# Hybrid encoder layer on one core: the router gathers part of the first expert's rows early, and makes the first weights later

## The chip, the core and the metric

One core of one Trainium2 chip runs the whole program in one launch. The time is the device time of that core in microseconds (us); lower is better.

## What is computed

The layer has one mixer (a state-space group and an attention group, joined by an output projection), a layer norm, and a mixture of 16 experts with another layer norm. The change lies between the first norm and the second expert. Cut to what matters (512 tokens, width 1024, experts 512 wide, 4 groups of 4 experts, 2 experts per token):

```python
h = layer_norm(alpha * x + mix, ln1_g, ln1_b)
g_val, g_idx = top_k(softmax(h @ rg_w + rg_b), 1)
e_logits = (einsum('td,gde->tge', h, re_w) + re_b)[g_idx]
e_val, e_idx = top_k(softmax(e_logits), 2)
weights = g_val * e_val / sum(e_val)
for e in range(16):
    act = silu(h @ w_gate[e]) * (h @ w_up[e])
    out = out + combine[:, e:e + 1] * (act @ w_down[e])
y = layer_norm(alpha * h + out, ln2_g, ln2_b)
```

## The kernel before

The 512 tokens are four tiles of 128 rows. PE (TensorE) runs nearly all the time; ACT (ScalarE), DVE (VectorE) and POOL (GpSimd) feed it and empty its results. PE's instructions keep the order of the code, and inside the router's block (from line 1305) those of DVE, ACT and POOL do as well; outside that block a scheduler sets the order on the three. Each engine takes its own queue in order, so that an instruction that waits holds all that stand behind it. SP issues the weights' DMAs, POOL those that gather and scatter rows.

**Router.** For each tile t `proj_half` finishes the output projection in two halves of 12 matmuls (line 805); `norm_stats`, `norm_gain` and `norm_bias` (lines 1150 to 1173) make the normed rows `hh[t]`. A tile in `NBV` (only tile 2) takes scale and bias in one DVE operation (line 1170), the others a scale on ACT and an addition on POOL (lines 1172 and 1173). `norm_store` writes the rows to two buffers in HBM, `hb` (read by the gathers) and `ub` (into which the experts add). `u_T` and `logits` transpose rows and multiply them by the router's weights (lines 1190, 1195). `choose` ranks groups and experts on DVE and leaves a mask `mskb`; `seat` counts with small matmuls how many tokens of each expert stand ahead of a token (lines 1251, 1252; result `place`), so that a token has a seat in its expert's tile of 128.

**First expert's rows.** For expert 0 the rows are not gathered from HBM but picked on the chip: `seat` makes for each tile a 128 x 128 matrix `pick[t]` that is 1 where a token has a seat (line 1256), and `picked` multiplies the rows by it, transposed, into two PSUM banks `px` (line 1266; 8 matmuls for each of the four tiles, each recorded twice, after a matmul that opens the bank, line 1264). `split` (lines 98, 99) makes of them the high and low halves `xgh` and `xgl` that the gate and up matmuls read.

**Lists and weights.** `weigh` makes every token's two weights (lines 1274 to 1297, DVE and two ACT operations) and writes them into `entry`. `seats_of` makes masks `se` for one expert (line 932) and `list_of` multiplies them by `entry` (line 940): two columns give the token numbers (`ix`, lines 945, 946), three the weights (`wc`, line 949). `call(e)` does this for an expert and gathers its rows (line 953). In the code before, the weights, expert 0's list with its weights, expert 1's weights and the counts `pcnt` (line 1379) are all made at the end of the router.

**Experts.** `gate_up` does 48 matmuls in four steps (lines 999 to 1001) on weight pieces that `wsplit` splits into `eh` (ACT, line 982) and `el` (DVE, line 983), four buffers of each; then silu on ACT (1009) and the product `ac` on DVE (1010), which includes the weight. While expert e runs, `call(e + 2)` stands after its third step. `act_T`, `down` and `finish` follow one expert later: `DOWN[0]` is empty, and expert 0's down projection runs in the pass of expert 1. Line 1007 of the code before begins the loop that makes `ac`.

Of the kernel before, what the change touches and what calls it, by code (L numbers as in the profile page):

```python
# [47 lines left out]
EARLY = 3  # L48
NBV = (2,)
PT = ("o", "s")  # L50
# [27 lines left out]
def hybrid_layer(ctx: ExitStack, tc: tile.TileContext, x, xT, wu, w16, bT, bz, bv, b16, cw, cb,  # L78
# [872 lines left out]

    def gather(ix, xg):
        G.indirect_dma_start(out=xg, out_offset=None, in_=hb,  # L953
                             in_offset=bass.IndirectOffsetOnAxis(ap=ix, axis=0),
                             bounds_check=S - 1, oob_is_err=False)

# [32 lines left out]
    def gate_up(e, xt_, tag="pj"):  # L989
# [17 lines left out]
        for j in range(2):  # L1007
            sg_, a_ = Q("sg"), Q("ac")
            A.activation(sg_, pg[:, j * 256:(j + 1) * 256], AF.Silu)
            V.scalar_tensor_tensor(a_, sg_, lists[e][1], pu[:, j * 256:(j + 1) * 256], op0=OP.mult, op1=OP.mult)  # L1010
            acts[e] += [a_[:, :P], a_[:, P:]]
# [30 lines left out]
    def finish(e, py, store=True):  # L1042
        yo = wide("x", "yo", NX, F32)
        A.activation(yo[:, :512], py[0], AF.Copy)
        if store:
            V.tensor_copy(yo[:, 512:], py[1])
        else:
            A.activation(yo[:, 512:], py[1], AF.Copy)
        if store:
            put(yo, lists[e][0])  # L1050
        return yo
# [190 lines left out]


    pick, px = {}, []

    def seat(t0, t1):
# [6 lines left out]
        V.scalar_tensor_tensor(place[:, t0:t1], pp_[:, t0:t1], 1.0, mskb[:, t0:t1], op0=OP.add, op1=OP.mult)  # L1253
        for t in range(t0, t1):
            pick[t] = xgs[0][:, t * P:(t + 1) * P]
            V.scalar_tensor_tensor(pick[t], seats, place[:, t, 0:1], onesf.to_broadcast([P, P]), op0=OP.is_equal, op1=OP.mult)

    def picked(ts, ks):

        for k in ks:  # L1260
            if k % 4 == 0 and len(px) == k // 4:
                px.append(bank("pj", "px"))

                T.matmul(px[-1], lhsT=identb, rhs=maskq[:, 0:1].to_broadcast([P, 512]), start=True, stop=False)
            for t in ts:
                T.matmul(px[k // 4][:, k % 4 * P:(k % 4 + 1) * P], lhsT=hh[t][:, k * P:(k + 1) * P], rhs=pick[t],
                         start=False, stop=(t == NT - 1 and k % 4 == 3))

    def weigh():
# [8 lines left out]
        for k in (1, 0):  # L1278
            V.scalar_tensor_tensor(oh[k], CH["rank"][:, :, 1:5], float(k), og, op0=OP.is_equal, op1=OP.mult)
            if k:  # L1280
# [4 lines left out]
                A.activation(r1, r1, AF.Exp)  # L1285
        yield
        V.tensor_reduce(gs, gx, axis=AX.X, op=OP.add)
# [17 lines left out]
    with tc.manual_schedule(engines=VECTOR):  # L1305
        for t in range(NT):
            ph_ = proj_half(t, 0)
            if t == 3:
                next(ph_)
                next(ph_)  # L1310
                u_T(2, 0)
                u_T(2, 1)
                norm_gain(2)
            drop(ph_)
            if t in DSP0:
# [9 lines left out]
            if t < 3:  # L1325
                if t == 2:
                    logits(1)
                    choose(0, 2)
                    next(ph_)
                    next(ph_)  # L1330
                    next(ph_)
                    seat(0, 2)
                drop(ph_)
                norm_stats(t)
                if t == 1:
                    logits(0)
                if t:
                    norm_store(t - 1, hb, G)
                    norm_store(t - 1, ub, G)
        next(ph_)  # L1340
        next(ph_)
        u_T(3, 0)
        drop(ph_)
        logits(2, range(3))
        u_T(3, 1)
        logits(3, range(4))
        norm_stats(3)
        norm_store(2, hb, G)
        norm_gain(3)
        norm_shift(3)  # L1350
        norm_bias(3)
        logits(3, range(4, 8))
        logits(2, range(3, 8))
        choose(2, 4)
        picked((0,), range(KC))
        seat(2, 4)
        norm_store(3, hb, G)
        picked((1,), range(KC))
        picked((2, 3), range(4))
        dsp[0, 2] = wsplit(raw[0, 2])  # L1360
        wg_ = weigh()
        next(wg_)
        xt_ = [wide("x", n, NX).rearrange("p (k s) -> p k s", s=P) for n in ("xgh", "xgl")]
        for hf in range(2):
            if hf:
                picked((2, 3), range(4, 8))
            split(*(t_[:, hf * 4:hf * 4 + 4] for t_ in xt_), px[hf].rearrange("p (k s) -> p k s", s=P))
# [9 lines left out]
    pn = bank("s", "pcnt")[:, :16]  # L1377
    for tt in range(NT):
        T.matmul(pn, lhsT=onesb, rhs=mskb[:, tt], start=(tt == 0), stop=(tt == NT - 1))
    V.tensor_reduce(cnt_i, pn, axis=AX.X, op=OP.max)  # L1380
    rt.close()
    at = {}
    for e in range(NEXP):
# [172 lines left out]
```

## Time and profile before

| | |
|---|---|
| median of 3 runs | 651.36 us (651.08 to 651.52) |
| the profiled execution's own time | 650.47 us |
| its span | 648.5 us |
| PE busy | 584.4 us, 90% of the span |
| DVE, ACT, POOL busy | 532.4, 414.1, 256.4 us |
| granted PE clock, mean | 0.96 of full speed |
| router's last part and first expert's gate and up | 286 to 339 us of the span |
| experts | from there to about 626 us |

The profile is of one execution; its own time is the span and what lies around it, 2.0 us. Idle time of an engine is told with what ended it ("6.08 <-DVE se" means that the engine stood 6.08 us and went on when DVE had made `se`). The granted clock of PE is 1.00 at 2.4 GHz and 0.50 at 1.2 GHz. A busy PE need not be PE at its best: its matmuls overlap, so the distance between two starts is what one costs.

### The profile page before, as it was taken

To read this page: it belongs to the slowest core of one execution; us is meant where nothing else is said; L and a number is where in the kernel's file an instruction comes from. 1 tells how busy PE (TensorE), PEld (TensorE's weight loads), DVE (VectorE), ACT (ScalarE), POOL (GpSimd) and SP (SyncE) were. 2 spreads that over 40 slices of the span, in tenths; PEclk is the share of its full clock that TensorE was granted. 3 is DMA by queue.
4 is the path that set the end of the run, shared out by engine and by line. 5 is a ranking of instruction groups with operands and counts; after the bars stand their busy time and mean duration, and the time that the engine had idled before them with its cause. 6 is when DMAs were issued, how large, how long until landed. Compare 5 with 4: busy or idle time off the path is not lost.

```text
span 648.5 us, 9222 instructions
## 1 busy us (share of the span) xinstructions
PE 584.4 (90%) x3061; PEld 482.8 (74%) x3061; DVE 532.4 (82%) x871; ACT 414.1 (64%) x628; POOL 256.4 (40%) x262
## 2 busy tenths in 40 slices
PE   5887996999999989998699999999999999999960
PEld 4677786889777768787677888888888888877840
DVE  3986789688668797678759999999999999999672
ACT  5443454443578875342168888888888888887760
POOL 5527623733453531034624223343333332211282
PEclk9997997999999999999889999999999999999975
DMA  7411112211211075985598999999999999991442
GB/s 261 136 66 67 65 66 66 81 66 46 86 67 65 33 252 185 388 308 192 187 348 293 367 359 361 374 366 348 346 343 364 351 347 369 331 336 43 123 170 83
DMA packets 61559, 141.09 MB, mean 218 GB/s; under 512 B 9919, under 2 KB 9935, under 8 KB 61504
## 3 DMA queue, kind: packets, MB, share of 16 engines
q1 hardware_dynamic: 55168, 125.79, 54.0%
q0 software_dynamic: 6336, 14.63, 7.7%
q8 instruction: 26, 0.43, 0.3%
q14 instruction: 29, 0.24, 0.1%
HBM read 134.17 MB, written 14.68 MB: 230 GB/s over the span
## 4 chain that ended last, share of the span: by engine, by line
PE 61%; DVE 14%; ACT 8%; issue 6%; DMA 5%; POOL 4%; SPq 0%; POOLq 0%; ACTq 0%; DVEq 0%
PE pw L805 6%; PE pg L999 5%; PE pg L1001 4%; PE pu L999 4%; PE pg L1000 4%; PE py L1033 4%; PE pu L1001 4%; PE pu L1000 4%; PE py L1035 4%; PE py L1034 4%; PE pjT L245 3%; PE pjR L269 3%; DVE acc L432 3%; PE pxg L975 2%; DMA wr<-in_wu 2%
## 5 line engine op out<-in xcount | busy, mean ns | idle before, releaser
L982 ACT ACTIVATE eh<-wf 128x1024 fp32r<-128x1024 f32 x192 | 203.2, 1061 | 56.7 <-PE pg L1001 21.7
L229 POOL TENSOR_TENSOR wl<-wr,wh 128x512 fp32r<-128x512 f32 x40 | 56.8, 1444 | 43.4 <-ACT wh L224 40.6
L953 POOL DMA_INDIRECT xg<-hb,ix x15 | 20.9, 1393 | 110.5 <-PE pg L1001 105.3
L1039 POOL DMA_INDIRECT ub<-yo,ix x15 | 27.6, 1841 | 88.2 <-ACT at L98 49.8
L1033 PE MATMUL py<-eh,at 128*128 128x512 f32 x128 | 53.0, 414 | 2.1 <-ACT at L98 1.8
L999 PE MATMUL pg<-eh,xgh 128*128 128x512 f32 x128 | 53.1, 415 | 0.8 <-ACT xgh L98 0.8
L1035 PE MATMUL py<-eh,at 128*128 128x512 f32 x128 | 51.1, 399 | 0.0
L1001 PE MATMUL pg<-eh,xgl 128*128 128x512 f32 x128 | 50.7, 396 | 0.0
L999 PE MATMUL pu<-eh,xgh 128*128 128x512 f32 x128 | 50.4, 394 | 0.0
L1001 PE MATMUL pu<-eh,xgl 128*128 128x512 f32 x128 | 50.1, 391 | 0.0
L932 POOL TENSOR_SCALAR se<-seats,place 128x128 bf16<-128x128 f32 x60 | 47.1, 794 | 1.2 <-DVE place L1253 0.6
L245 PE MATMUL pjT<-xh,wh 128*128 128x512 f32 x112 | 46.3, 414 | 1.3 <-DVE kl L669 1.3
L269 PE MATMUL pjR<-wh,xh 128*128 128x256 f32 x128 | 39.3, 307 | 8.8 <-ACT acc L424 7.6
L245 PE MATMUL pjT<-xh,wl 128*128 128x512 f32 x112 | 44.1, 394 | 0.0
L245 PE MATMUL pjT<-xl,wh 128*128 128x512 f32 x112 | 44.0, 393 | 0.0
L269 PE MATMUL pjR<-wl,xh 128*128 128x256 f32 x128 | 38.0, 297 | 0.0
L269 PE MATMUL pjR<-wh,xl 128*128 128x256 f32 x128 | 37.9, 296 | 0.0
L269 PEld LDWEIGHTS pjR<-wh,xh 128*128 128x128 f32 x128 | 26.6, 208 | 9.4 <-ACT acc L424 8.0
L1033 PEld LDWEIGHTS py<-eh,at 128*128 128x128 f32 x128 | 24.7, 193 | 8.0 <-ACT at L98 2.0
L1035 PEld LDWEIGHTS py<-eh,at 128*128 128x128 f32 x128 | 24.6, 192 | 5.8 <-DVE at L99 0.6
L1001 PEld LDWEIGHTS pg<-eh,xgl 128*128 128x128 f32 x128 | 24.3, 190 | 5.9 <-DVE xgl L99 0.4
L999 PEld LDWEIGHTS pu<-eh,xgh 128*128 128x128 f32 x128 | 24.3, 190 | 5.2
(960 smaller groups left out, 1774.4 us busy)
## 6 DMA issues: line engine op xcount, KB each, us to landing
wf<-in_w_up SPq DMA_DIRECT2D x64, 512.0 KB
wf<-in_w_gate SPq DMA_DIRECT2D x64, 512.0 KB
wf<-in_w_down SPq DMA_DIRECT2D x60, 512.0 KB
wr<-in_wu SPq DMA_DIRECT2D x22, 512.0 KB
wor<-in_w_out SPq DMA_DIRECT2D x8, 512.0 KB
hh<-in_x SPq DMA_DIRECT2D x4, 512.0 KB
hb<-hh POOLq DMA_DIRECT2D x4, 512.0 KB, 3.1
ub<-hh POOLq DMA_DIRECT2D x4, 512.0 KB, 5.3
```

The costliest lines, as they stand in the source:

```text
L229: G.tensor_tensor(l_[:, j], wr_[:, j], h_[:, j].bitcast(F32), op=OP.subtract)
L245: T.matmul(pt, lhsT=w_[:, k % 4, m * P:(m + 1) * P], rhs=x_[k], start=(i == 0), stop=(i == 23))
L269: T.matmul(pt, lhsT=x_[k][:, t * P:(t + 1) * P], rhs=w_[:, k % 4, :], start=(i == 0), stop=(i == 23))
L805: T.matmul(pw, lhsT=m_[k][:, ts_], rhs=wo[k][w_][:, c_], start=(i == 0), stop=(i == 11))
L932: eng.tensor_scalar(r[t], seats, place_(t), None, op0=OP.is_equal)
L982: A.activation(h_, src, AF.Copy)
L999: T.matmul(pt, lhsT=h_[:, k], rhs=wh_[:, f], start=(k == 0), stop=False)
L1000: T.matmul(pt, lhsT=h_[:, k], rhs=wl_[:, f], start=False, stop=False)
L1001: T.matmul(pt, lhsT=l_[:, k], rhs=wh_[:, f], start=False, stop=(k == KC - 1))
L1033: T.matmul(pt, lhsT=h_[:, f], rhs=wh_[:, c_], start=(f == 0), stop=False)
L1035: T.matmul(pt, lhsT=l_[:, f], rhs=wh_[:, c_], start=False, stop=(f == 3))
L1039: G.indirect_dma_start(out=ub, out_offset=bass.IndirectOffsetOnAxis(ap=ix, axis=0), in_=yo, in_offset=None, bounds_check=S - 1, oob_is_err ...
```

## The change

- Tiles 1, 2 and 3 take scale and bias on DVE (`NBV`); only tile 0 still uses ACT and POOL.
- `seat(0, 2)` stands one half later, after the first 3 matmuls of tile 3, and no longer makes picks. New `gather_first` makes a list of the tokens of tiles 0 and 1 that expert 0 takes (two masks on DVE, two small matmuls, two DVE operations) and gathers those rows from `hb` into `xgs[0]`; the rows of tiles 0 and 1 are stored to HBM earlier.
- `px_open` opens both banks ahead of the last logits. `px_add` adds the gathered rows by a multiplication with the identity (8 matmuls for both tiles together instead of 16), then those of tiles 2 and 3 by picks as before (16). These picks now lie in `xgs[1]`.
- `weigh` moves behind `call(2)` in expert 0's `gate_up`; expert 0's list and the weights of experts 0, 1 and 2 and the counts move into expert 1's `gate_up` (`weights_of_first`). So `ac` of expert 0 is made without the weight, and `finish` multiplies it in.

```diff
-NBV = (2,)
+NBV = (1, 2, 3)
...
-    def gather(ix, xg):
-        G.indirect_dma_start(out=xg, out_offset=None, in_=hb,
+    def gather(ix, xg, n=S):
+        G.indirect_dma_start(out=xg, out_offset=None, in_=hb[:n],
...
-            V.scalar_tensor_tensor(a_, sg_, lists[e][1], pu[:, j * 256:(j + 1) * 256], op0=OP.mult, op1=OP.mult)
+            if e:
+                V.scalar_tensor_tensor(a_, sg_, lists[e][1], pu[:, j * 256:(j + 1) * 256], op0=OP.mult, op1=OP.mult)
+            else:
+                V.tensor_tensor(a_, sg_, pu[:, j * 256:(j + 1) * 256], op=OP.mult)
...
-        A.activation(yo[:, :512], py[0], AF.Copy)
-        if store:
+        A.activation(yo[:, :512], py[0], AF.Copy, scale=1.0 if e else lists[e][1])
+        if store and e == 0:
+            V.tensor_scalar(yo[:, 512:], py[1], lists[e][1], None, op0=OP.mult)
+        elif store:
...
-        for t in range(t0, t1):
-            pick[t] = xgs[0][:, t * P:(t + 1) * P]
-            V.scalar_tensor_tensor(pick[t], seats, place[:, t, 0:1], onesf.to_broadcast([P, P]), op0=OP.is_equal, op1=OP.mult)
...
+    def gather_first():
+        r = Q("se").bitcast(BF16)
+        pl = bank("s", "plist")[:, :2]
+        for t in range(2):
+            r_ = r[:, t * P:(t + 1) * P]
+            V.tensor_scalar(r_, seats, place[:, t, 0:1], None, op0=OP.is_equal)
+            T.matmul(pl, lhsT=r_, rhs=entry_of(0)(t)[:, 0:2], start=(t == 0), stop=(t == 1))
+        ix, if_ = lp.tile([P, 1], I32, name="ix", bufs=6), lp.tile([P, 1], F32, name="if_")
+        V.tensor_reduce(if_, pl, axis=AX.X, op=OP.add)
+        V.tensor_scalar(ix, if_, float(BIG), None, op0=OP.add)
+        gather(ix, xgs[0], 2 * P)
...
+    def px_add(rows, m, ks, last=False):
         for k in ks:
+            T.matmul(px[k // 4][:, k % 4 * P:(k % 4 + 1) * P], lhsT=rows[:, k * P:(k + 1) * P], rhs=m,
+                     start=False, stop=(last and k % 4 == 3))
+
+    def picks(t):
+        pick[t] = xgs[1][:, t * P:(t + 1) * P]
...
             if t == 3:
                 next(ph_)
+                seat(0, 2)
                 next(ph_)
                 u_T(2, 0)
                 u_T(2, 1)
                 norm_gain(2)
+                gather_first()
...
                     logits(1)
+                    norm_store(1, hb, G)
+                    norm_store(1, ub, G)
                     choose(0, 2)
-                    next(ph_)
-                    next(ph_)
-                    next(ph_)
-                    seat(0, 2)
...
         choose(2, 4)
-        picked((0,), range(KC))
+        px_add(xgs[0], identf, range(KC))
         seat(2, 4)
+        for t in (2, 3):
+            picks(t)
+        norm_bias(3)
         norm_store(3, hb, G)
-        picked((1,), range(KC))
-        picked((2, 3), range(4))
+        px_add(hh[2], pick[2], range(KC))
         dsp[0, 2] = wsplit(raw[0, 2])
-        wg_ = weigh()
-        next(wg_)
...
-                picked((2, 3), range(4, 8))
+            px_add(hh[3], pick[3], range(4 * hf, 4 * hf + 4), True)
...
-        drop(wg_)
-        lists[0] = list_of(lp, seats_of(lp, lambda t: place[:, t, 0:1], V), entry_of(0))
-        lists[1][1] = list_of(lp, lists[1][1], entry_of(1), tokens=False)[1]
...
+    def weights_of_first():
+        lists[0] = list_of(lp, seats_of(lp, lambda t: place[:, t, 0:1], G), entry_of(0))
+        for e in (1, 2):
+            lists[e][1] = list_of(lp, lists[e][1], entry_of(e), tokens=False)[1]
...
-            call(e + 2)
+            call(e + 2, bool(e))
+            if e == 0:
+                weigh()
+            if e == 1:
+                weights_of_first()
             drop(gu)
```

How the order of the instructions moves, at three places. The line numbers are those of the kernel that the rows are of: of the changed one, 1254 and 1255 are the seats (1251 and 1252 before), 1283 the picks (1266), 1013 expert 0's product and 1401 the counts.

First PE, from the seats of tiles 2 and 3 to expert 0's first gate matmul; `xg_3005` and `xg_3006` are `xgs[0]` and `xgs[1]`. Before:

```order
L1252 MATMUL ppos<-mskb,strictb 128x16
L1266 MATMUL px<-xg_3005,hh 128x128 x24
L940 LDWEIGHTS se
L940 MATMUL plist<-entry,se 128x2
...
L940 MATMUL plist<-entry,se 128x5
...
L940 MATMUL plist<-entry,se 128x3
...
L1379 MATMUL pcnt<-mskb,onesb 128x16
L999 MATMUL pg<-eh,xgh 128x512
```

And now:

```order
L1283 MATMUL px<-identf,xg_3005 128x128 x8
...
L1255 MATMUL ppos<-mskb,strictb 128x16
L1283 MATMUL px<-xg_3006,hh 128x128 x16
L940 LDWEIGHTS se
L940 MATMUL plist<-entry,se 128x2
...
L999 MATMUL pg<-eh,xgh 128x512
```

The lists with weights (5 and 3 columns) and the counts are gone from this place; expert 1's list of tokens (2 columns) still stands ahead of the gate matmuls.

Second PE in expert 1's `gate_up`, between its third and fourth step. Before:

```order
L1001 MATMUL pu<-eh,xgl 128x512
L940 LDWEIGHTS se
L940 MATMUL plist<-entry,se 128x5
...
L999 MATMUL pg<-eh,xgh 128x512
L1000 MATMUL pg<-el__3696,xgh 128x512
```

And now:

```order
L1001 MATMUL pu<-eh,xgl 128x512
L940 LDWEIGHTS se
L940 MATMUL plist<-entry,se 128x5
...
L940 MATMUL plist<-entry,se 128x3
...
L1401 LDWEIGHTS onesb
L1401 MATMUL pcnt<-mskb,onesb 128x16
...
L999 MATMUL pg<-eh,xgh 128x512
L1000 MATMUL pg<-el__3702,xgh 128x512
```

One list of 4 matmuls (expert 3's) became two lists of 4 with token numbers and weights, two of 4 with weights alone, and 4 matmuls for the counts.

Third DVE, ahead of expert 0's two products. Before:

```order
L983 TENSOR_TENSOR el__3617<-wf,eh 128x1024
L945 TENSOR_REDUCE if__3530<-plist 128x1
L949 TENSOR_REDUCE wc<-plist 128x1
L946 TENSOR_SCALAR ix<-if__3530 128x1
L983 TENSOR_TENSOR el__3627<-wf,eh 128x1024
L1010 SCALAR_TENSOR_TENSOR ac<-sg,wc,pu 128x256
```

And now:

```order
L983 TENSOR_TENSOR el__3586<-wf,eh 128x1024
L945 TENSOR_REDUCE if__3480<-plist 128x1
L1315 CAST entry<-arena_3181 128x64
L983 TENSOR_TENSOR el__3596<-wf,eh 128x1024
L946 TENSOR_SCALAR ix<-if__3480 128x1
L1317 TENSOR_TENSOR arena_3181<-arena_3181,entry 128x64
L1315 CAST entry<-arena_3181 128x64
L1317 TENSOR_TENSOR arena_3181<-arena_3181,entry 128x64
L1315 CAST entry<-arena_3181 128x64
L1013 TENSOR_TENSOR ac<-sg,pu 128x256
```

The last operations of `weigh` now stand between the weight splits and the first product, and six more of them further up in the same stretch.

## Rows read from the trace of the kernel before

**Rows 1.** Windows: stretch, length, busy (count) of PE, PEld, DVE, ACT, POOL, clock, DMA, GB/s.
```profile
308.00:313.00 5.00, 5.00 (x31) 4.79 (x30) 3.82 (x9) 0.17 (x1) 4.08 (x5) 0.52 0.64 249
313.00:318.00 5.00, 5.00 (x49) 4.92 (x47) 2.98 (x9) 1.03 (x4) 1.66 (x2) 1.00 0.63 212
318.00:325.50 7.50, 0.97 (x15) 0.69 (x13) 6.06 (x24) 1.53 (x2) 5.61 (x8) 0.84 0.44 162
325.50:330.00 4.50, 4.50 (x15) 3.53 (x13) 0.68 (x2) 1.06 (x1) 1.00 (x2) 0.51 1.01 383
330.00:339.00 9.00, 9.00 (x45) 7.20 (x44) 7.03 (x9) 7.21 (x8) 1.00 (x1) 1.00 0.97 324
```

**Rows 2.** Timeline of PE, last picks to first gate: start, us, instruction, wait.
```profile
311.91 6.04 PE L1266 MATMUL px<-xg,hh 128*128 128x128 f32 x48
...
317.79 0.24 PE L940 MATMUL plist<-entry,se 128*128 128x2 bf16 x4
...
324.11 0.82 PE L940 MATMUL plist<-entry,se 128*128 128x5 bf16 x8 [6.08 <-DVE se L932]
...
325.46 0.77 PE L999 MATMUL pg<-eh,xgh 128*128 128x512 f32 x1
```

**Rows 3.** Timeline of DVE in that gap: start and end of the weights.
```profile
320.70 0.16 DVE L1287 TENSOR_REDUCE arena<-arena 128x4 f32<-128x16 f32 x1
...
323.65 0.93 DVE L932 TENSOR_SCALAR se<-seats,place 128x128 bf16<-128x128 f32 x4
```

**Rows 4.** Timeline of PE, gate and up of expert 0: half rate, full rate, end.
```profile
326.03 0.63 PE L1000 MATMUL pg<-el__3041,xgh 128*128 128x512 f32 x1
...
326.46 0.63 PE L1001 MATMUL pg<-eh,xgl 128*128 128x512 f32 x1
...
330.59 0.39 PE L1000 MATMUL pg<-el__3357,xgh 128*128 128x512 f32 x1
...
330.82 0.40 PE L1001 MATMUL pg<-eh,xgl 128*128 128x512 f32 x1
...
338.56 0.39 PE L1001 MATMUL pu<-eh,xgl 128*128 128x512 f32 x1
```

**Rows 5.** Timeline of PE, first pick matmuls of the last stretch.
```profile
307.45 0.59 PE L1264 MATMUL px<-maskq,identb 128*128 128x512 bf16 x1
...
309.97 1.91 PE L1266 MATMUL px<-xg,hh 128*128 128x128 f32 x8
```

**Rows 6.** Timeline of PE at the first seats, tile 2.
```profile
294.61 0.17 PE L1252 MATMUL ppos<-mskb,strictb 128*128 128x16 bf16 x1 [1.62 <-DVE mskb L1240]
...
297.66 0.48 PE L805 MATMUL pw<-woh,m 128*128 128x512 f32 x1
```

**Rows 7.** Timeline of DVE: group choice beside POOL, gain of tile 2, two picks.
```profile
292.17 2.17 DVE L1238 SCALAR_TENSOR_TENSOR arena<-arena,onesf 128x8 f32<-128x8 f32 x1
...
297.94 1.28 DVE L1166 SCALAR_TENSOR_TENSOR hh<-hh,mv,l1g 128x1024 f32<-128x1024 f32 x1 [0.40 <-PE phT L1190]
...
312.32 0.73 DVE L1256 SCALAR_TENSOR_TENSOR xg<-seats,place,onesf 128x128 f32<-128x128 f32 x2
```

**Rows 8.** Timeline of POOL: one store of rows, four list masks.
```profile
309.96 0.57 POOL L1176 DMA_DIRECT2D hb<-hh  x1 [0.30 <-POOL hh L1173]
...
339.42 3.45 POOL L932 TENSOR_SCALAR se<-seats,place 128x128 bf16<-128x128 f32 x4
```

**Rows 9.** Tile view of xg: the gathers, and their time to landing.
```profile
L953 POOL DMA_INDIRECT xg<-hb,ix x15: 1337/1350/1956, 319.9 to 567.5; - x15
...
DMA to landing us min/median/max: 5.8/7.5/8.2
```

**Rows 10.** Timelines, end of expert 0: first product of DVE, then PE waiting.
```profile
339.07 0.48 DVE L1010 SCALAR_TENSOR_TENSOR ac<-sg,wc,pu 128x256 f32<-128x256 f32 x1 [0.69 <-PE pu L1001]
...
341.69 0.44 PE L1016 MATMUL pat<-identf,ac 128*128 128x128 f32 x2 [1.64 <-DVE ac L1010]
```

**Rows 11.** Waits view, 340 to 620 us: who waited for whom: us, times, longest us.
```profile
ACT eh L982 <- DMA wf<-in_w_down: 1.7, 3, 1.1
```

More of the change, by code (lines that the diff above doesn't have):

```diff
@@ L950, in list_of @@
         return ix, wc
-    def gather(ix, xg):
-        G.indirect_dma_start(out=xg, out_offset=None, in_=hb,
+    def gather(ix, xg, n=S):
+        G.indirect_dma_start(out=xg, out_offset=None, in_=hb[:n],
                              in_offset=bass.IndirectOffsetOnAxis(ap=ix, axis=0),
-                             bounds_check=S - 1, oob_is_err=False)
+                             bounds_check=n - 1, oob_is_err=False)
     lists, dsp, acts = {}, {}, {}
@@ L1241, in choose @@
                                c["og"][:, :, :, None].to_broadcast([P, n, 4, 4]), op0=OP.is_lt, op1=OP.mult)
-    pick, px = {}, []
     def seat(t0, t1):
@@ L1253, in seat, with px_open @@
         V.scalar_tensor_tensor(place[:, t0:t1], pp_[:, t0:t1], 1.0, mskb[:, t0:t1], op0=OP.add, op1=OP.mult)
-        for t in range(t0, t1):
-            pick[t] = xgs[0][:, t * P:(t + 1) * P]
-            V.scalar_tensor_tensor(pick[t], seats, place[:, t, 0:1], onesf.to_broadcast([P, P]), op0=OP.is_equal, op1=OP.mult)
-    def picked(ts, ks):
-        for k in ks:
[L1261 to L1267, printed above, removed]
+    px, pick = [], {}
+    def gather_first():
[9 more added lines that the diff above has]
+        gather(ix, xgs[0], 2 * P)
+    def px_open():
+        px.append(bank("pj", "px"))
+        T.matmul(px[-1], lhsT=identb, rhs=maskq[:, 0:1].to_broadcast([P, 512]), start=True, stop=False)
+    def px_add(rows, m, ks, last=False):
+        for k in ks:
+            T.matmul(px[k // 4][:, k % 4 * P:(k % 4 + 1) * P], lhsT=rows[:, k * P:(k + 1) * P], rhs=m,
+                     start=False, stop=(last and k % 4 == 3))
+    def picks(t):
+        pick[t] = xgs[1][:, t * P:(t + 1) * P]
+        V.scalar_tensor_tensor(pick[t], seats, place[:, t, 0:1], onesf.to_broadcast([P, P]), op0=OP.is_equal, op1=OP.mult)
     def weigh():
@@ L1285, in weigh @@
                 A.activation(r1, r1, AF.Exp)
-        yield
         V.tensor_reduce(gs, gx, axis=AX.X, op=OP.add)
@@ L1336, in hybrid_layer @@
                     logits(0)
-                if t:
-                    norm_store(t - 1, hb, G)
-                    norm_store(t - 1, ub, G)
+                    norm_store(0, hb, G)
+                    norm_store(0, ub, G)
         next(ph_)
@@ L1344, in hybrid_layer @@
         logits(2, range(3))
+        px_open()
         u_T(3, 1)
@@ L1348, in hybrid_layer @@
         norm_store(2, hb, G)
+        norm_shift(3)
         norm_gain(3)
-        norm_shift(3)
-        norm_bias(3)
         logits(3, range(4, 8))
+        px_open()
         logits(2, range(3, 8))
         choose(2, 4)
-        picked((0,), range(KC))
+        px_add(xgs[0], identf, range(KC))
         seat(2, 4)
+        for t in (2, 3):
+            picks(t)
+        norm_bias(3)
         norm_store(3, hb, G)
-        picked((1,), range(KC))
-        picked((2, 3), range(4))
+        px_add(hh[2], pick[2], range(KC))
         dsp[0, 2] = wsplit(raw[0, 2])
-        wg_ = weigh()
-        next(wg_)
         xt_ = [wide("x", n, NX).rearrange("p (k s) -> p k s", s=P) for n in ("xgh", "xgl")]
         for hf in range(2):
-            if hf:
-                picked((2, 3), range(4, 8))
+            px_add(hh[3], pick[3], range(4 * hf, 4 * hf + 4), True)
             split(*(t_[:, hf * 4:hf * 4 + 4] for t_ in xt_), px[hf].rearrange("p (k s) -> p k s", s=P))
@@ L1372, in hybrid_layer @@
         dsp[0, 3] = wsplit(raw[0, 3])
-        drop(wg_)
-        lists[0] = list_of(lp, seats_of(lp, lambda t: place[:, t, 0:1], V), entry_of(0))
-        lists[1][1] = list_of(lp, lists[1][1], entry_of(1), tokens=False)[1]
[L1377 to L1381, printed above, removed]
+    def weights_of_first():
+        lists[0] = list_of(lp, seats_of(lp, lambda t: place[:, t, 0:1], G), entry_of(0))
+        for e in (1, 2):
+            lists[e][1] = list_of(lp, lists[e][1], entry_of(e), tokens=False)[1]
+        pn = bank("s", "pcnt")[:, :16]
+        for tt in range(NT):
+            T.matmul(pn, lhsT=onesb, rhs=mskb[:, tt], start=(tt == 0), stop=(tt == NT - 1))
+        V.tensor_reduce(cnt_i, pn, axis=AX.X, op=OP.max)
+        rt.close()
     at = {}
```

## The prediction

> **What bounds the kernel now.** I read the windows first, then PE's timeline in the stretch they point to, then the timelines of the engines that PE waits for there. Almost everywhere PE is full; the hole is the stretch from 318 to 325.5 us, where PE is busy 0.97 of 7.5 us while DVE works 6.06 [rows 1]. PE's timeline tells why: the last picks end near 317.8, expert 1's list follows, then PE stands 6.08 us until DVE has made the masks `se`, does two lists and the counts, and starts expert 0's first gate matmul at 325.46 [rows 2]. DVE spends that time on the second half of `weigh`, from 320.70 to the masks that end at 324.6 [rows 3]. None of this is needed by the gate matmuls: it feeds the weight that is multiplied in behind them. The reader should see a wait for an operand that is only due 13 us later.
>
> The hole has a second price. From 325.5 to 330 the granted clock is 0.51, about 1.2 GHz, after PE had stood in the gap; from 330 it is 1.00 [rows 1]. Two starts are 0.43 us apart at the low level (326.03 and 326.46) and 0.23 at the high one (330.59 and 330.82) [rows 4]. About ten matmuls fall into the slow part.
>
> **The change part by part.** The terms are differences on PE up to the end of expert 0's gate and up, 338.8 us [rows 4], and a little behind it.
>
> *First seats.* Before, PE stands 1.62 us for `mskb` [rows 6], in part because one operation of `choose` takes 2.17 us beside POOL's bias [rows 7]. Now the seats come 3 matmuls into tile 3, when the mask is ready. The new list makes another wait: it stands on PE behind tile 2's transposes, and on DVE behind the gain of tile 2, which itself waits for those transposes and takes 1.28 us [rows 7]; two masks (a quarter of 0.93 each [rows 3], 0.5 together) follow. So PE stands about 1.9 us there, and is 0.3 us later than before at 297.66 [rows 6]. Bias on DVE costs 1.28 us twice; one lies beside 12 projection matmuls, the other behind the picks (below).
>
> *Picks.* Both bank openers (0.59 for the first, with its tail [rows 5]) now stand among the logits: some 0.4 us later again, so that the gathered rows are first needed at 308.1 instead of the picks at 307.45 [rows 5]. The gather is issued on POOL when its list is ready, at 298.4 by this reckoning, and 15 gathers landed 5.8 to 8.2 us after their issue [rows 9]: by 306.6 at the latest, so nothing waits. Eight matmuls are recorded as 16 rows; eight such rows start over 1.71 us at the low clock (309.97 to the seats at 311.68, 1.91 with the tail [rows 5]), so 16 cost 3.4. On DVE the first operations of `weigh` now stand between those of `choose`; this adds some 0.8 us to the mask and is covered by these 3.4 us (uncovered, it would cost the 0.8). Then the seats, a wait for place and the first of two picks (0.73 together [rows 7]) of about 0.8 us, which the old order hid behind tile 1's picks, and 32 rows for tiles 2 and 3 from 312.6. The 32 cost 6.8 us at the low clock and 3.4 at the high one. Before, the clock rose near here: 0.52 from 308 to 313 and 1.00 from 313 to 318 [rows 1]. So the picks end between 316.0 and 319.4.
>
> *Gate's start.* PE's next instruction is expert 1's list, and its masks come from POOL. There they stand behind the store of tile 3's rows, and that behind the bias of tile 3 on DVE: picks to 312.9, bias 1.28, to 314.2; store 0.57 [rows 8], to 314.8; four masks, 3.45 us beside a busy DVE [rows 8] and less beside an idle one, say 3.2: 318.0; list 0.24 [rows 2]. The first gate matmul then starts at 318.2 if the picks ran at the high clock, at 319.7 if not. I take 318.2, since the clock rose at that place before: **-7.3 us** (-5.8 at the other end). All of `eh` and `el` that it needs at once exist already; the pieces behind are 30 buffers ahead, and ACT stood only 1.7 us for a `w_down` piece in all the experts [rows 11].
>
> *Clock.* The ten slow matmuls cost 0.20 us more each: **-2.0 us** if the clock stays high, 0 if not. I take -2.0: PE's hole shrinks to under 2 us, and 1.62 us of standing at 294 did not lower it.
>
> *DVE in expert 0.* The second half of `weigh`, 3.1 us without the masks [rows 3], moves beside expert 0's gate matmuls. From 330 to 339 DVE is busy 7.03 of 9 us [rows 1], so about 2.0 of 3.1 fit in and 1.1 delay the products `ac`, for which PE already waits 1.64 us [rows 10]: **+1.1 us** (0 to 3.1).
>
> *Weights in expert 1.* Sixteen list matmuls and four for the counts use two PSUM banks in turn, so that the third list waits until DVE has read the first. Before, two lists and the counts took 1.35 us from 324.11 to 325.46 with DVE free [rows 2]; now there are four lists (two more round trips) and a weight split of 1.2 us may stand ahead on DVE. One list stood there already, at about 0.2. I take **+2.1 us** (1.1 to 3.9).
>
> *No cost.* Expert 0's product without the weight and its multiplication in `finish` use operations of the same size. Expert 0's masks move to POOL: four more, 3.45 us, in a stretch where POOL works 1.0 of 9 us [rows 1]; they are due some 3 us after they end, and past that PE would wait. Expert 1's gather is issued near 320.5 and lands by 328.7; its rows are due at 329.4, and PE then waits for `ac` anyway. Expert 2's token list is read on DVE some 2 us later than before; its gather still has some 7 us to spare. The experts' later passes are as before and shift as a whole.
>
> Sum: -7.3 - 2.0 + 1.1 + 2.1 = **-6.1 us**, so 644.4 for the profiled execution (650.47), whose time is 0.9 under the median of 651.36. On the median: **645.3 us**. About 0.2% (1.3 us) is what a measurement of this kernel can tell from no change.
>
> **Rivals.**
>
> *Low clock over picks and first gate matmuls.* PE now works in pieces between 308 and 318. If the clock rises only after the gate has begun, the kernel loses the 1.5 us of the later start and the 2.0: -6.1 + 3.5 = -2.6, 648.8. For it: 0.52 from 308 to 313 [rows 1]; against: it rose under the same kind of matmul. 20%.
>
> *The wait only changes its owner.* PE then waits at expert 1's list for POOL instead of DVE: store and masks take longer than reckoned, because POOL reads SBUF beside DVE's splits. The slowest pace in rows, 3.45 for four, is used up already; twice that starts the gate at 321.6: -6.1 + 3.4 = -2.7, 648.7. 7%.
>
> *Late weights free.* `weigh` and the lists of expert 1 fit into time in which PE waits anyway: -6.1 - 3.1 = -9.2, 642.2. For it: PE already stands 1.64 at `ac` [rows 10]. 13%.
>
> *The gather lands late.* PE's queue holds at the gathered rows, and the second seats, the picks and the gate behind them. Every us past 308.1 is one; landing at 314.2, 15.8 us after issue, gives no change (651.4). Against it: 8.2 at most in 15, while DVE was near its limit [rows 9]. 5%.
> The Trainium skill (SBUF — State Buffer, "A bandwidth-pool intuition that's wrong") speaks against the gather: a DMA that POOL issues, 620 ns alone, took about 3100 beside a DVE copy, since its descriptors wait for a port that DVE holds. Applied to the longest issue here, 1.96 us, five times is an estimate of 9.8 us, which puts the landing near 314.4 and the time at 651.6; the landings in this trace show no such stretch.
>
> *Low clock through the whole gate and up, slower.* With the late start (-6.1 + 1.5) every gate matmul at the low level costs 0.20 more: 48 cost 9.6 and give 651.36 + 5.0 = 656.4. It decides from 23 slow matmuls on. Against it: ten were enough before [rows 1, 4]. 5%.
>
> **How the numbers follow.** The forecast has 50%, with 643.8 to 646.8 as its own range. The range 642.2 to 648.9 takes in the free weights, the low clock and the change of owner, and the bounds of the terms; it leaves out the last two rivals and the tails. Faster by over 0.2%: 50 + 20 + 7 + 13 = 90%; within: 5% (late gather); slower: 5%.
>
> **What would show it.** Right: no PE wait over 2 us between the last pick and the first gate matmul, which starts near 318 at 0.23 us spacing; PE's wait of about 1.9 us at the first list; a gather landed before 308; PE some 3 us idle before expert 1's gate, and some 2 us in expert 1 among the lists. Wrong: a wait on the gathered rows, a gate at 0.43 spacing beyond ten matmuls, or an end of the experts that has not moved by what the gate's start has.

## The result, and the profile after

The changed kernel takes a median of 641.88 us (641.58 to 646.04, 4 runs) against 651.22 us (650.34 to 651.52, 4 runs) of the kernel before on the same chip: ratio 0.9874, interval 0.9832 to 0.9915. A second set, on another chip (D1 below), gave 642.50 us (640.13 to 645.73, 6 runs) and a ratio of 0.9903 (0.9881 to 0.9924). The forecast was 645.3 with a range from 642.2 to 648.9: the sign and the kind of gain were right, by the first set the size was about a third too small, and the first median lies 0.3 us under the range, the second inside it.

The profiled execution took 641.58 us with a span of 639.5. Its windows, with the columns of [rows 1]:

```profile
298.00:302.00 4.00, 4.00 (x15) 3.18 (x13) 2.88 (x5) 0.00 (x0) 1.13 (x1) 0.58 0.57 188
302.00:316.00 14.00, 12.17 (x105) 11.49 (x104) 9.74 (x27) 3.95 (x7) 4.37 (x8) 1.00 0.64 233
316.00:327.20 11.20, 11.20 (x54) 9.04 (x54) 10.16 (x22) 8.74 (x11) 6.90 (x9) 1.00 0.77 236
327.20:330.00 2.80, 1.65 (x14) 1.18 (x12) 2.73 (x7) 2.80 (x5) 2.69 (x3) 1.00 1.04 419
```

The hole is gone: the gate and up of expert 0 fill 316.0 to 327.2 at a clock of 1.00, where before PE stood until 325.46 and then ran ten matmuls at 0.51 [rows 1, 2]. In these windows the only low clock is at 298 to 302.

The timeline of PE, from the first list to expert 1's gate, answers to [rows 2, 4 to 6, 10]:

```profile
288.08 1.96 PE L1201 MATMUL plg<-gw,hT 128*128 128x20 f32 x16 [0.31 <-ACT hT L1197]
...
296.98 0.37 PE L1269 MATMUL plist<-entry,se 128*128 128x2 bf16 x2 [1.58 <-DVE se L1268]
297.21 0.48 PE L805 MATMUL pw<-woh,m 128*128 128x512 f32 x1
...
308.00 2.03 PE L1283 MATMUL px<-identf,xg 128*128 128x128 f32 x16
...
311.15 3.81 PE L1283 MATMUL px<-xg,hh 128*128 128x128 f32 x32 [0.76 <-DVE xg L1288]
...
315.31 0.18 PE L940 MATMUL plist<-entry,se 128*128 128x2 bf16 x1 [0.32 <-POOL se L932]
...
315.89 0.18 PE L940 MATMUL plist<-entry,se 128*128 128x2 bf16 x1 [0.40 <-POOL se L932]
...
315.93 0.48 PE L999 MATMUL pg<-eh,xgh 128*128 128x512 f32 x1
316.25 0.39 PE L1000 MATMUL pg<-el__3041,xgh 128*128 128x512 f32 x1
316.48 0.39 PE L1001 MATMUL pg<-eh,xgl 128*128 128x512 f32 x1
...
329.78 0.44 PE L1019 MATMUL pat<-identf,ac 128*128 128x128 f32 x2 [1.03 <-DVE ac L1013]
329.97 0.48 PE L999 MATMUL pg<-eh,xgh 128*128 128x512 f32 x1
```

Four shorter waits stand where one of 6.08 us stood: 1.58 at the early list, 0.76 at the second picks, and 0.32 and 0.40, 0.72 together, for POOL's masks at expert 1's list. The wait of 1.62 at the first seats [rows 6] is gone too. The gate matmuls start 0.23 apart from the second on. One place is new, expert 1 between its third and fourth step (PE):

```profile
338.25 0.36 PE L940 MATMUL plist<-entry,se 128*128 128x5 bf16 x8
339.60 0.51 PE L940 MATMUL plist<-entry,se 128*128 128x3 bf16 x8 [0.99 <-DVE wc L949]
340.11 0.25 PE L1401 MATMUL pcnt<-mskb,onesb 128*128 128x16 bf16 x4
340.21 0.47 PE L999 MATMUL pg<-eh,xgh 128*128 128x512 f32 x1
```

POOL, at the gate's start (compare [rows 8]), and the tile view of the gathers from 290 to 345 us (compare [rows 9]):

```profile
312.77 0.53 POOL L1182 DMA_DIRECT2D hb<-hh  x1 [5.96 <-DVE hh L1176]
313.33 5.66 POOL L932 TENSOR_SCALAR se<-seats,place 128x128 bf16<-128x128 f32 x8
319.16 1.74 POOL L953 DMA_INDIRECT xg<-hb,ix  x1 [0.17 <-POOL se L932]
```

```profile
L953 POOL DMA_INDIRECT xg<-hb,ix x4: 1071/1121/1741, 298.6 to 339.9; - x4
...
DMA to landing us min/median/max: 4.6/7.1/8.4
```

The early gather is issued at 298.6; its landing, at most 8.4 us later, is ahead of the first use at 308.00, and no wait names it.

**Where the time went.** Absolute times mislead here: the changed execution is already 0.74 us ahead at the logits of tile 1 (288.08 against 288.82), and this difference arises within the first 30 us of the span, where the code is the same. So I count stages from PE's first `plg` matmul near 288 to 290 us, and beside them how long the clock was low between that mark and the gate, worked out from the clock of one window over it (twice the missing share, times its length; the clock has two digits, so about 0.3 us either way).

| stage on PE, us | before | after | after, second set |
|---|---|---|---|
| mark to expert 0's first gate matmul | 36.64 | 27.85 | 26.31 |
| of it at the low clock | 9.5 | 3.3 | 0 |
| gate and up of expert 0 | 13.33 | 11.23 | 11.24 |
| from there to expert 1's gate | 3.09 | 2.81 | 2.85 |
| expert 1's gate and up | 11.19 | 13.09 | 13.07 |
| sum | 64.25 | 54.98 | 53.47 |

From expert 2 on both run with the same stages: with the 0.74 us of the start the changed execution is 10.0 us ahead at expert 2's first gate matmul and 10.1 at the end of the last expert's; 1.1 of it is lost behind that (span -9.0).

### The profile page after: what moved, and what is told of

Same layout as the page of the kernel before. It is cut to its first block, busy times and chain, and to the rows that moved or that the text cites. A ratio compares the mean times of both kernels' runs of the same rounds, so it can differ in the third digit from the quotient of the medians.

```text
span 639.5 us, 9197 instructions
## 1 busy us (share of the span) xinstructions
PE 579.6 (91%) x3050; PEld 478.3 (75%) x3051; DVE 528.2 (83%) x871; ACT 411.8 (64%) x626; POOL 254.9 (40%) x265
## 4 chain that ended last, share of the span: by engine, by line
PE 60%; DVE 15%; ACT 8%; issue 6%; POOL 5%; DMA 4%; SPq 0%; POOLq 0%; ACTq 0%; DVEq 0%
PE pw L805 6%; PE pg L999 5%; PE pg L1001 4%; PE pg L1000 4%; PE py L1036 4%; PE py L1038 4%; PE py L1037 4%; PE pu L999 4%; PE pu L1001 4%; PE pu L1000 4%; PE pjT L245 3%; DVE acc L432 3%; DMA wr<-in_wu 2%; PE pxg L975 2%; POOL wl L229 1%
## 5 line engine op out<-in xcount | busy, mean ns | idle before, releaser
L932 POOL TENSOR_SCALAR se<-seats,place 128x128 bf16<-128x128 f32 x64 | 51.1, 808 | 0.5
L1036 PEld LDWEIGHTS py<-eh,at 128*128 128x128 f32 x128 | 24.5, 191 | 8.7 <-ACT at L98 2.8
L1001 PEld LDWEIGHTS pu<-eh,xgl 128*128 128x128 f32 x128 | 24.0, 188 | 5.2
```

What stands on the lines that cost most here:

```text
L932: eng.tensor_scalar(r[t], seats, place_(t), None, op0=OP.is_equal)
L1001: T.matmul(pt, lhsT=l_[:, k], rhs=wh_[:, f], start=False, stop=(k == KC - 1))
L1036: T.matmul(pt, lhsT=h_[:, f], rhs=wh_[:, c_], start=(f == 0), stop=False)
```

## The experiments

Every kernel was timed in five rounds beside the kernel before, in three groups: A and B of four kernels, then D with the changed kernel itself. Ratios are to the kernel before in the same group.

| kernel | median us | ratio | interval | mark to gate | low clock in it |
|---|---|---|---|---|---|
| A1 late weights alone | 641.85 | 0.9882 | 0.986 to 0.9903 | 27.69 | 3.3 |
| A2 early gather alone | 650.46 | 1.0014 | 1.0 to 1.0028 | 37.93 | 16.7 |
| A3 no early gather | 639.87 | 0.9844 | 0.9827 to 0.9861 | 29.06 | 7.0 |
| A4 biases back | 644.83 | 0.9917 | 0.9893 to 0.994 | 29.00 | 3.5 |
| B1 list ahead of gain | 639.0 | 0.9825 | 0.9807 to 0.9843 | 25.78 | 3.6 |
| B2 one bank | 647.24 | 0.996 | 0.9945 to 0.9974 | 27.71 | 3.3 |
| B3 masks ahead of store | 642.98 | 0.9893 | 0.9876 to 0.991 | 26.70 | 3.2 |
| B4 all three | 644.04 | 0.9904 | 0.9885 to 0.9923 | 24.95 | 3.5 |
| D1 changed kernel again | 642.5 | 0.9903 | 0.9881 to 0.9924 | 26.31 | 0 |
| D2 lists spread | 642.46 | 0.9877 | 0.986 to 0.9895 | 29.46 | 10.0 |
| D3 spread, list ahead of gain | 639.17 | 0.9827 | 0.9806 to 0.9848 | 24.64 | 0 |
| D4 spread, no early gather | 639.44 | 0.9834 | 0.9817 to 0.985 | 27.42 | 3.3 |

The last two columns are of the one profiled execution; they are why a single trace can't rank these kernels. A3 and D4 have the same router, and their marks to gate differ by 1.6 us with 3.7 us of low clock between them.

### A: which part of the change carries the gain

**A1, late weights alone.** Router, picks and biases of the kernel before; `weigh`, the lists and the factor in `finish` as in the changed one.

```diff
-        wg_ = weigh()
-        next(wg_)
...
-        drop(wg_)
-        lists[0] = list_of(lp, seats_of(lp, lambda t: place[:, t, 0:1], V), entry_of(0))
-        lists[1][1] = list_of(lp, lists[1][1], entry_of(1), tokens=False)[1]
...
-            call(e + 2)
+            call(e + 2, bool(e))
+            if e == 0:
+                weigh()
+            if e == 1:
+                weights_of_first()
```

> The kernel before, with the late weights alone: weigh beside expert 0's gate, the lists of weights in expert 1, the factor in finish; picks, biases and seats as before. Theory (the hole was only the wait for the weights): the gate's first matmul follows the list of expert 1 at about 318.2 instead of 325.46 (-7.3); if the clock stays high its first ten matmuls give back 2.0; the lists in expert 1 cost 1.75 as in the changed kernel; DVE costs nothing beside expert 0. Sum -7.5, about 643.7. Rival (the gather and the high clock over the picks carry half of the gain): -4 or less, 647 and over, with the gate's start at 0.43 us spacing.

0.9882: the whole gain of the change, to within the intervals, and 7.6 us by the medians of its group, which is the theory's -7.5. PE goes from the picks into expert 1's list and the gate without a wait, at the high clock:

```profile
311.70 5.61 PE L1271 MATMUL px<-xg,hh 128*128 128x128 f32 x48
317.14 0.24 PE L940 MATMUL plist<-entry,se 128*128 128x2 bf16 x4
317.25 0.48 PE L999 MATMUL pg<-eh,xgh 128*128 128x512 f32 x1
317.57 0.39 PE L1000 MATMUL pg<-el__3041,xgh 128*128 128x512 f32 x1
```

The mark to gate is 27.69, that of the changed kernel 27.85, both with 3.3 us of low clock. The rival falls. The theory put the gate 29.4 us behind the mark (318.2 less 288.82); it comes 1.7 earlier, since the theory's end of the picks came from an execution with more low clock. For the same reason the two profiled executions, A1's and that of the kernel before, are 9.4 us apart at expert 2's gate, which is more than the medians show.

**A2, early gather alone.** The changed router, with the weights made at its end again.

```diff
         dsp[0, 3] = wsplit(raw[0, 3])
+        weigh()
+        lists[0] = list_of(lp, seats_of(lp, lambda t: place[:, t, 0:1], V), entry_of(0))
+        lists[1][1] = list_of(lp, lists[1][1], entry_of(1), tokens=False)[1]
```

> The changed kernel, but with weigh, expert 0's list and the weights of expert 1 and the counts at the router's end again, and the weight in ac; early gather, picks of two tiles and biases on DVE stay. Theory: the picks end near 314.8 as in the changed kernel, and PE then waits for DVE, which has 3 us of weigh, a split and four masks to do: gate's start near 323.5 instead of 325.46, -2 and with it 649 (the slow first matmuls of the gate remain). Rival (the earlier end of the picks is handed on whole): gate's start near 321.5, -4 or more, 647 and less.

1.0014, no gain at all; the rival falls and the theory's -2 as well. PE spends 6.88 instead of 6.08 us at the old wait:

```profile
318.96 0.24 PE L940 MATMUL plist<-entry,se 128*128 128x2 bf16 x4
326.08 0.92 PE L940 MATMUL plist<-entry,se 128*128 128x5 bf16 x8 [6.88 <-DVE se L932]
327.41 0.28 PE L1393 MATMUL pcnt<-mskb,onesb 128*128 128x16 bf16 x4 [0.40 <-DVE wc L949]
327.54 0.77 PE L999 MATMUL pg<-eh,xgh 128*128 128x512 f32 x1
```

Two things stand behind this. In this execution PE comes to the list no earlier than before, 29.35 us after the mark against 28.97, with a clock of 0.83 on the way against 0.88. And the edit puts the whole of `weigh` behind expert 1's list, while the kernel before has its first six operations ahead of `split`. Here they lie in the hole (DVE, the first of the six before and in A2):

```profile
314.11 0.22 DVE L1274 TENSOR_REDUCE arena<-lg 128x20 f32<-128x80 f32 x1
```

```profile
321.87 0.23 DVE L1290 TENSOR_REDUCE arena<-lg 128x20 f32<-128x80 f32 x1
```

From the last `xgl` to the masks DVE takes 5.27 us instead of 4.34. So about 0.9 us of A2's wait is the edit's own, and what the early gather would give with the first half of `weigh` at its old place is not shown.

**A3, no early gather.** Tiles 0 and 1 picked on the chip, in the changed order.

```diff
-                gather_first()
+                for j in range(2):
+                    picks(j, 0)
...
-        px_add(xgs[0], identf, range(KC))
+        for t in range(2):
+            px_add(hh[t], pick[t], range(KC))
```

> The changed kernel without the early gather: tiles 0 and 1 are picked on chip too (two picks on DVE at the place of the two masks, 16 matmuls in 32 records instead of 8 in 16), no list on PE at 297. Theory (at the high clock the gather saves 16 records, 1.9 us, and costs 1.58 us of PE waiting at its list and 1.2 us of low clock behind that wait): -0.9, 641.0 and at most the same. Rival (the gather is worth what it saves at the low clock that ran there before, 3.4 us, since the wait costs nothing that isn't lost elsewhere): 643.8 to 645.3.

639.87, as the theory had it (641.0 or less) and under the rival's 643.8: the gather does not pay for its list. Its interval lies under that of the second set of the changed kernel, though on another chip; the first set's interval overlaps it (D4 and D2 make the same comparison on one chip). The waits at the second picks and for POOL's masks are in A3 as well, 0.76 and 0.72, so that they belong to the new order and not to the gather.

**A4, biases back.** `NBV = (2,)`.

> The changed kernel with the biases of tiles 1 and 3 on ACT and POOL again (scale about 1.1 us, addition 2.4 us, instead of 1.28 us on DVE). Theory (the bias of tile 3 stands ahead of the store and of expert 1's masks on POOL, which PE waits for at the gate's start): the masks and the first gate matmul come about 2.2 us later: 644.1, and POOL named at PE's wait. Rival (bias on either engine is hidden): 641.9.

644.83 fits the theory's number, but its interval meets that of the changed kernel, and the trace names another cause. POOL's addition of tile 3 now runs beside `choose`, as before the change, and is over before the masks are due. What is late is a DVE operation on 8 elements (timelines of DVE, POOL, PE):

```profile
308.48 2.34 POOL L1179 TENSOR_TENSOR hh<-hh,l1b 128x1024 f32<-128x1024 f32 x1 [2.40 <-ACT hh L1178]
...
308.87 1.98 DVE L1244 SCALAR_TENSOR_TENSOR arena<-arena,onesf 128x8 f32<-128x8 f32 x1
```

```profile
311.12 0.17 PE L1255 MATMUL ppos<-mskb,strictb 128*128 128x16 bf16 x1 [1.78 <-DVE mskb L1246]
```

In the changed kernel the same operation takes 0.16 us:

```profile
309.69 0.16 DVE L1244 SCALAR_TENSOR_TENSOR arena<-arena,onesf 128x8 f32<-128x8 f32 x1
```

It ends with POOL's addition (308.87 + 1.98 = 310.85; 308.48 + 2.34 = 310.82), and the one of the first pair of tiles did the same, 2.21 us beside an addition of 2.40. PE pays 1.78 at the second seats. So the bias on DVE is worth something, but at `choose`, not at POOL's masks.

### B: can the three new waits go

**B1, list ahead of the gain.**

```diff
-                norm_gain(2)
                 gather_first()
+                norm_gain(2)
```

> The changed kernel with gather_first ahead of the gain of tile 2, so that the two masks stand ahead of it on DVE. Theory (PE's 1.58 us at the list is DVE's order alone, and the low clock from 298.5 to 302 follows from that wait): no wait at the list, projections at 0.23 us spacing throughout, -1.6 -1.2 = -2.8, 639.1. Rival (the low clock falls somewhere in this stretch whatever the wait): low clock again, at the list's place or over the picks, -1.6 or less, 640.3 and over.

639.0, ratio 0.9825: the wait is gone, and the time as the theory said, but in part by luck. Of its -2.8, 1.2 were for a clock that stays high, and with no wait at the list a low stretch stands further on (timeline of PE, then the window from 306 to 310), as the rival has it. From the mark the gate is 2.1 us earlier than in the first profile of the changed kernel, at about the same low clock.

```profile
295.39 0.37 PE L1269 MATMUL plist<-entry,se 128*128 128x2 bf16 x2
```

```profile
306.00:310.00 4.00, 3.24 (x25) 3.11 (x24) 2.52 (x11) 0.22 (x1) 0.00 (x0) 0.66 0.56 223
```

**B2, one bank** for the lists and the counts of expert 1's pass.

```diff
+        pl = bank("s", "plist")
-        lists[0] = list_of(lp, seats_of(lp, lambda t: place[:, t, 0:1], G), entry_of(0))
+        lists[0] = list_of(lp, seats_of(lp, lambda t: place[:, t, 0:1], G), entry_of(0), pl=pl)
...
-            lists[e][1] = list_of(lp, lists[e][1], entry_of(e), tokens=False)[1]
+            lists[e][1] = list_of(lp, lists[e][1], entry_of(e), tokens=False, pl=pl[:, 16 * e:])[1]
...
-        pn = bank("s", "pcnt")[:, :16]
+        pn = pl[:, 64:80]
```

> The changed kernel with the four lists of expert 1's pass (its three late ones and the counts) in one PSUM bank, at different columns, instead of two banks in turn. Theory (PE's 0.99 us there waits for DVE to read the first list, since the bank is needed again): the wait goes, -1.0, 640.9. Rival (PE then waits for POOL's masks of expert 0 or for the next weight split instead, or the wait covered one that comes later): within 0.4 of the changed kernel.

Neither: 647.24, four to six us slower than the changed kernel by the ratios (0.996 against 0.9903 and 0.9874). Each list now waits until DVE has read the one ahead of it, although the columns differ, so that one wait became three, and the clock fell behind them:

```profile
341.18 0.24 PE L940 MATMUL plist<-entry,se 128*128 128x3 bf16 x4 [1.24 <-DVE wc L949]
342.52 0.24 PE L940 MATMUL plist<-entry,se 128*128 128x3 bf16 x4 [1.10 <-DVE wc L949]
343.02 0.26 PE L1402 MATMUL plist<-mskb,onesb 128*128 128x16 bf16 x4 [0.25 <-DVE wc L949]
```

```profile
343.00:348.40 5.40, 5.38 (x17) 4.11 (x17) 1.14 (x2) 1.33 (x2) 2.73 (x5) 0.50 1.05 389
```

Expert 1's gate and up take 17.08 instead of 13.09: 1.6 of the 4.0 are waits (2.59 against 0.99), the rest matmuls 0.43 apart. So 1.6 us more of waiting in a full stretch cost 4.0 in this execution.

**B3, masks ahead of the store.**

```diff
             picks(t)
+        se1 = seats_of(lp, lambda t: place[:, t, 1:2], G)
         norm_bias(3)
...
-        call(1, False)
+        call(1, False, se1)
```

> The changed kernel with expert 1's four masks ahead of the store of tile 3's rows on POOL (place is ready at 310.6, the bias of tile 3 at 312.5). Theory (the waits of 0.32 and 0.40 us at expert 1's list are POOL's order alone): both waits go and the gate starts 0.7 us earlier, 641.2; the store 2 us later holds nothing, since expert 1's gather is issued behind it anyway. Rival (PE then waits for the split xgl of the first half, which ends at 315.43, or for eh): -0.2 or less.

642.98, no gain. Both waits for masks are gone, and the mark to gate is 1.2 shorter at the same low clock, but the store I called harmless isn't: the eight masks of experts 1 and 2 stand ahead of it, the gather waits for the stored rows, and PE for the gather (timelines of POOL and PE):

```profile
316.98 0.59 POOL L1182 DMA_DIRECT2D hb<-hh  x1
322.35 1.09 POOL L953 DMA_INDIRECT xg<-hb,ix  x1 [4.77 <-DMA hb<-hh]
```

```profile
330.07 1.09 PE L975 MATMUL pxg<-identf,xg 128*128 128x128 f32 x8 [1.77 <-DMA xg<-hb,ix]
```

At expert 2's first gate matmul nothing of the 1.2 is left: 61.5 us after the mark against 61.7.

**B4, all three.**

> The three edits together: list ahead of the gain, one bank, masks ahead of the store. Theory (three separate waits on PE): -2.8 -1.0 -0.7 = -4.5, 637.4. Rival (an engine behind them, DVE's chain to place or the splits, is next, or the low clock comes back): -2 or less, 640 and over.

644.04: the best start of the gate in this group (24.95), and it loses more than that behind it, by the two mechanisms of B2 and B3, both in its trace (1.38 us at `pxg`, 1.25, 1.10 and 0.25 at the lists, and behind them a clock of 0.58 from 340.3 to 344.0).

### D: the clock, and a version that beats both

**D1, the changed kernel again.**

> The changed kernel as it is, beside the three others on one chip. Theory (the low clock of some 4 us between 298 and 314 and the first 30 us of the span vary between executions, not the sum of the terms): ratio to the kernel before 0.986 to 0.990, a low stretch again of about 4 us, at 298 to 302 or over the rows and picks at 306 to 312. Rival (the low stretch at 298 to 302 is the answer to PE's 1.58 us at the list): it lies at 298 to 302 again.

Both miss the clock; the ratio lies at the edge of the theory's. The wait at the list is the same 1.58 us, and behind it the clock stays high up to the gate (timeline of PE and windows):

```profile
297.97 0.37 PE L1269 MATMUL plist<-entry,se 128*128 128x2 bf16 x2 [1.58 <-DVE se L1268]
298.20 0.48 PE L805 MATMUL pw<-woh,m 128*128 128x512 f32 x1
298.52 0.40 PE L805 MATMUL pw<-wol,m 128*128 128x512 f32 x1
```

```profile
298.00:302.00 4.00, 3.98 (x20) 3.22 (x21) 2.46 (x8) 0.00 (x0) 1.13 (x1) 1.00 0.53 147
302.00:316.00 14.00, 12.16 (x104) 11.47 (x104) 11.14 (x30) 4.50 (x7) 4.93 (x9) 1.00 0.73 259
```

The same kernel, 1.54 us faster to the gate than in the first profile, which is half of that one's 3.3 us at the low clock. Its six runs go roughly with the mean clock: 640.13 us at 0.970, 645.73 at 0.959.

**D2, lists spread** (counts and expert 1's weights behind the first step, the weights of expert 2 and expert 0's list behind the second; `weights_of_first` as a generator, stepped in the loop; the expectation counts these steps one too few).

```diff
+        se0 = seats_of(lp, lambda t: place[:, t, 0:1], G)
+        yield
         pn = bank("s", "pcnt")[:, :16]
...
+        lists[1][1] = list_of(lp, lists[1][1], entry_of(1), tokens=False)[1]
+        yield
+        lists[2][1] = list_of(lp, lists[2][1], entry_of(2), tokens=False)[1]
+        lists[0] = list_of(lp, se0, entry_of(0))
```

> The changed kernel with the lists of expert 1's pass spread over its steps: counts and weights of expert 1 after no step, weights of expert 2 and expert 0's list after the first, expert 3's list after the third as in every pass; never more than two lists at one place, with the two PSUM banks. Theory (PE's 0.99 us is the third list's wait for a bank that DVE reads late, behind a weight split): no wait over 0.3 us among them, -1.0 to -1.5 against the changed kernel. Rival (the lists then wait for POOL's masks of expert 0 or for entry): a wait of 1 us or more at plist again, no gain.

In the trace as the theory has it: no wait, and expert 1's gate and up take 11.92 instead of 13.09.

```profile
335.82 0.26 PE L1399 MATMUL pcnt<-mskb,onesb 128*128 128x16 bf16 x4
335.94 0.24 PE L940 MATMUL plist<-entry,se 128*128 128x3 bf16 x4
336.04 0.48 PE L999 MATMUL pg<-eh,xgh 128*128 128x512 f32 x1
...
338.87 0.35 PE L940 MATMUL plist<-entry,se 128*128 128x3 bf16 x8
339.09 0.48 PE L999 MATMUL pg<-eh,xgh 128*128 128x512 f32 x1
```

The times don't settle it: 642.46 against 642.50, ratios 0.9877 and 0.9903 with intervals that overlap.

**D3, spread with the list ahead of the gain** (the edits of D2 and B1).

> The spread lists together with gather_first ahead of the gain of tile 2. Theory (two separate waits of PE, 1.58 and 0.99 us): -2.6 to -3.0 against the changed kernel, ratio near 0.982. Rival (one of the two only moves the time into another wait): as the better of the two alone, -1.6.

639.17, ratio 0.9827, and its interval lies under that of the changed kernel on the same chip (0.9806 to 0.9848 against 0.9881 to 0.9924). With B1 it has the lowest ratio of all, though the intervals of A3 and D4 overlap both. B1 alone, in its own group, has the same ratio, so what the spread adds is not shown by the times.

**D4, spread without the gather** (the edits of D2 and A3).

> The spread lists and no early gather: all four tiles are picked on chip. Theory (where its list makes PE wait for nothing, the gather is worth the 16 records that it saves, 1.9 us at the high clock and up to 3.4 at the low one): 1.2 to 2.5 slower than the spread lists with the list first, and as fast as or faster than the spread lists alone. Rival (the gather is worth nothing at all): as fast as with the list first, within 0.6.

639.44: not told apart from D3 (0.9834, intervals overlap), as the rival has it. Even the 1.9 us that the theory puts on the 16 records at the high clock don't show in the medians. The theory's second half holds, and it is the plainest test of the early gather as the change has it: D2 and D4 differ in that alone, on one chip, and D4's interval lies under D2's (0.9817 to 0.985 against 0.986 to 0.9895), by 3.0 us of the medians; how much of that is the clock stays open (0.963 to 0.968 in D2's runs, 0.967 to 0.969 in D4's). Whether the gather is worth something once its list makes no wait, the traces don't settle. D4 has 3.3 us of low clock before the gate, D3 none; less half of it, D4's mark to gate would be 25.8 against 24.64. But the same reckoning gives 24.5 for D2, where the same router took 26.31 in D1 with no low clock, so that it is good to some 2 us only.

## Why the prediction was right, and where it fell short

*The hole.* Right: A1 takes the late weights alone and has the whole gain; A2 keeps them at the router's end and has none, with some 0.9 us of its own against it.

*First seats.* Right. 1.58 us of wait (forecast 1.9), and the next projection matmul 9.13 us after the mark against 8.84, the +0.3 of the text.

*Picks and the gate's start, forecast -7.3.* This is the step that failed in size: -8.8 from the mark, -10.3 in the execution without a low stretch. "16 cost 3.4" took the price of the low clock from the rows of that place; from start to start they took 1.87 at the high one (308.00 to 309.87). The low stretch came at 298 to 302 instead, so that only 0.5 us of this is left at the end of the second picks, 26.7 us after the mark against 27.2 at the earliest by the forecast. The larger part, 1.1, is "3.2: 318.0", four masks stacked behind the store from 314.8 on: they started at 313.33 behind an earlier bias, took 2.5 us, not 3.2 (PE's list follows at 315.89), and the gate came 1.1 us behind the picks, not 2.2. The early gather I priced within that sum, and no run shows a gain from it in this place. The 16 records it saves are worth 1.9 us; its list alone takes back 1.58 of waiting, and the kernels without it are as fast or faster (A3), and faster on the same chip (D4 against D2). That A1 reaches the gate as soon as the changed kernel is a balance: it has the 1.62 at the first seats and 16 records more, and not the waits of 1.58, 0.76 and 0.72.

*Clock, -2.0.* Right: gate and up went from 13.33 to 11.23, and took 11.2 to 11.5 in every trace with late weights.

*DVE in expert 0, +1.1.* Wrong: -0.3. By the rows, I counted DVE's room from 330 to 339 only, and left out the slow part ahead of it, where it worked 0.68 of 4.5 us [rows 1]. DVE is now busy 10.16 of 11.20 us and PE's wait at `ac` is 1.03, shorter than before [rows 10].

*Weights in expert 1, +2.1.* Right: 13.09 against 11.19 is +1.9, with the wait for the bank as described; B2 made it longer, D2 took it away.

*The sum.* -8.8 -2.1 -0.3 +1.9 = -9.3 against the forecast's -6.1; 2.9 of the 3.2 lie in the two steps named. That this is also the difference of the first medians (9.3) is in part luck: the second set's stages sum to -10.8 and its medians differ by 7.5, since its profiled execution was the fastest of six. The rival "late weights free" stood at -9.2, close to the first median, by another road: `weigh` was free beside expert 0, the lists were not, and the earlier gate made up for them.

*The gather.* It landed in time, as forecast: PE waits for its rows in no kernel (the waits of B3 and B4 are for expert 1's). The sentence on the Trainium skill (SBUF — State Buffer, "A bandwidth-pool intuition that's wrong") gave 9.8 us for an issue stretched five times; the longest issue above, at 319.16, took 1.74 us beside a DVE at 10.16 of 11.20 us, and none in any run took over 2.11, so no run here shows that stretch.

*Open.* What the low stretch between 298 us and the gate follows. It came in the same kernel with and without, and with and without the wait at the list.

## What to carry to other kernels

When an engine waits, first ask which of the things made in the wait the next instruction needs: moving the others to the stage that uses them was worth the whole gain here, while A2, which was to send the engine earlier to the same wait, gained nothing. A new list, store or mask on the way costs by whom it stands ahead of, in its own queue and one hand-over further (B3). And compare single traces stage by stage from a common mark, with the low-clock time beside each, before ascribing one or two us to an edit.

## What the runs showed of the hardware

- A DVE operation on 8 elements took 0.16 us alone and 1.98 and 2.21 beside POOL's addition of 128x1024, and ended with it to within 0.03. The Trainium skill (SBUF — State Buffer, "SBUF: two separate sides") has it that DVE operations with two SBUF inputs and POOL operations that read SBUF take a shared pair of ports in turn, each for its whole length; this trace agrees. By that, what counts is not how long a small operation is, but what POOL is in the middle of.
- The clock fell to the low level in stretches at different places of the same code: at 298 to 302 in one execution of the changed kernel, nowhere between the mark and the gate in another. The runs of one kernel spread over 5 us (640.13 to 645.73), with the mean clock from 0.970 to 0.959.
- Waits of 1.6 us more in the full stretch of B2 cost 4.0, since the matmuls behind them ran at half rate for 5.4 us. B4 has the same three waits and a low stretch behind them; no other trace has those three, or a low stretch, in expert 1's pass.
